# Four of six residual updates of the seven-product down projections sent through ScalarE and an accumulating transfer

## The chip, the core and the metric

The kernel runs on one core of a Trainium2 chip. A core has five engines that each work through a queue of their own in order: TensorE (PE in the profile; its weight loads are PEld), VectorE (DVE), ScalarE (ACT), GpSimd (POOL) and SyncE (SP). They wait for each other through semaphores, and 16 DMA engines move data beside them. The metric is the device time of one execution in microseconds, smaller is better.

## What is computed

A two-layer decoder trunk on 512 tokens of width 1024, all in float32. Each layer is a half-step feed-forward network, a mixer (gated linear attention in layer 0, stick-breaking attention in layer 1), and another half-step feed-forward network, so there are four feed-forward networks:

```
def swiglu(h, w_gate, w_up, w_down):
    return (jax.nn.silu(h @ w_gate) * (h @ w_up)) @ w_down

for i in range(DEPTH):                       # DEPTH = 2
    x = x + 0.5 * swiglu(rmsnorm(x, ffn1_norm[i]), ...)
    x = x + mixer(rmsnorm(x, mix_norm[i]))
    x = x + 0.5 * swiglu(rmsnorm(x, ffn2_norm[i]), ...)
return rmsnorm(x, final_norm)                # D_MODEL = 1024, D_FF = 2816, SEQ = 512
```

What the change touches is `x = x + 0.5 * (... @ w_down)`.

## The kernel before

**Data.** The residual x stays on the chip for the whole run as eight tiles `xs[0]` to `xs[7]`, 128 features by 512 tokens each (`x_81` to `x_88` in the order of instructions). To keep float32 accuracy, every operand of a product is split into a high part (`wh`, `hh`, ..., made by a cast on ScalarE, L538) and a low part (`wl`, `hl`, ..., made by a subtraction on VectorE, L539), and every product is three matmuls: high by high, low by high, high by low.

**Seven products.** The 2816 hidden features are cut into 11 slices of 256 and these into five groups; groups 1, 2 and 3 go through `seven_down`, a two-by-two block scheme with seven products in place of eight (Strassen's, in Winograd's form). The four output blocks of a pair of residual tiles `xs[m]` (lower) and `xs[m + 4]` (upper), each 128 by 256 (a half of the tokens), are (0,0), (0,1), (1,0) and (1,1): `up` picks the tile, `col` the half. One block of work (one m) runs seven products, each of 9 matmuls of 128 by 256 where the group has three slices (n = 3). They accumulate in three PSUM tiles, `ws` (ps_w), `zs` (ps_z) and `qs` (ps_q), and after each of six of the products a partial sum is added to a residual block:

| product (matrix name) | adds into PSUM | then updates x block |
|---|---|---|
| 1 b11 | ws (copied to zs by ScalarE, L843) | none |
| 2 t1 | qs | (1,1) from qs |
| 3 t2 | ws | (0,1) from ws |
| 4 b21 | zs | (0,0) from zs |
| 5 t3 | ws | (1,1) from ws |
| 6 b22 | qs | (0,1) from qs |
| 7 t4 | ws | (1,0) from ws |

Products 3, 5 and 7 add on top of the same `ws`, so each of them must wait until the value before it has been read out. Before, all six updates are `add`, one VectorE instruction `x = 0.5 * ps + x` (L831). For product 5 ScalarE first copies `ws` to a spare tile `u3` in SBUF (L869, `u` in the profile), so that product 7 can go on, and VectorE adds from the copy.

Each of four networks has three such groups of four values of m: 48 blocks, 288 updates. In the last network the third group has n = 2 and runs two m at a time (6 matmuls a product); the other 44 blocks are alike. The scheme for the gate and up products (`seven`, PE L1164) is of the same kind and shares the spare-tile tag `c`.

**Order.** The order on each engine is not that of the code. A `Planner` walks all instructions with a price for each, simulates the five queues and writes a fixed order for each engine. TensorE takes the first instruction in code order that can start within 30 ns, otherwise the one that can start soonest; VectorE and ScalarE take what is due first; POOL keeps the order of the code. A transfer is priced by these lines, as 2050 ns plus its bytes divided by 318 per ns (2462 ns for 128 KB):

```
        if "DMA" in kind:
            total = max((s[1] * s[3] for s in sizes), default=1) * 4
            return 2050.0 + total / 318.0, total / 318.0
```

POOL is nearly unused: some fills, and ten transfers (the gate weights `gr` and `w`, constants `tri`, `lf`, `negm`, the last norm's gain `fin`). All weights are loaded by transfers that SP issues (L504). Tiles of a tag are recycled among its `bufs` buffers: the writer of a tile waits until the last reader of the one that had the buffer is done.

Of the kernel before, what the change touches and what calls it, by code (L numbers as in the profile page):

```python
# [11 lines left out]
F32 = mybir.dt.float32  # L12
# [3 lines left out]
AF = mybir.ActivationFunctionType  # L16
ALU = mybir.AluOpType
PSUM = bass.MemoryType.PSUM

P = 128  # L20
# [409 lines left out]
def turns(t):  # L430

    return t.rearrange("p (two n) -> p n two", two=2)


def flat(ps):

    return ps.rearrange("p (n two) -> p two n", two=2)


def pair(t):  # L440

    return t.rearrange("p (two n) -> p two n", two=2)
# [3 lines left out]
def decoder(ctx: ExitStack, tc: tile.TileContext, a: dict, out: bass.AP):  # L446
    nc = tc.nc
# [12 lines left out]
    def psum(name, tag=None):  # L460
        if tag is None:
            tag = order[turn_[0] % 8]
            turn_[0] += 1
        return pp.tile([P, T], F32, tag=tag, bufs=banks[tag], name=name)
# [11 lines left out]
    xs = [xp.tile([P, T], F32, name=f"x{k}") for k in range(KD)]  # L476
# [311 lines left out]
    def seven_down(pool, w, r0, hs, part, n, per):  # L788

        H = T // 2
        W_ = per * P
        lower, upper = (
            Chunk(w[r0 : r0 + 2 * n * P, c : c + W_].rearrange("(f p) c -> p f c", p=P), 2 * n, W_)
            for c in (part * W_, 512 + part * W_)
        )
        lower.few = upper.few = True
        v = {}

        def halves():

            lo, up = (c.load().rearrange("p (c two) d -> p two c d", two=2) for c in (lower, upper))
            return lo[:, 0], lo[:, 1], up[:, 0], up[:, 1]

        def sums_12(_):
            a11, _, a21, a22 = halves()
            s = v["s12"] = pool().tile([P, 2 * n, W_], F32, tag="s", bufs=4, name="s12")
            nc.vector.tensor_tensor(out=s[:, 0:n], in0=a21, in1=a22, op=ALU.add)
            nc.vector.tensor_tensor(out=s[:, n:], in0=s[:, 0:n], in1=a11, op=ALU.subtract)  # L810
            return s

        def sums_34(_):
            a11, a12, a21, _ = halves()
            s = pool().tile([P, 2 * n, W_], F32, tag="s", bufs=4, name="s34")
            nc.vector.tensor_tensor(out=s[:, 0:n], in0=a11, in1=a21, op=ALU.subtract)
            nc.vector.tensor_tensor(out=s[:, n:], in0=a12, in1=v["s12"][:, n:], op=ALU.subtract)
            return s

        def prod(ps, w, k0, m, b, first):  # L820
            for c in range(n):
                bh, bl = (turns(t) for t in hs[c][b])
                wh, wl = (t[:, k0 + c, m * P : (m + 1) * P] for t in w)
                for i, (l_, r_) in enumerate(((wh, bh), (wl, bh), (wh, bl))):
                    nc.tensor.matmul(  # L825
                        ps, l_, r_, start=first and c + i == 0, stop=c == n - 1 and i == 2, skip_group_check=True
                    )

        def add(m, up, col, ps):
            x = pair(xs[part * per + m + 4 * up][:, col * H : col * H + H])  # L830
            nc.vector.scalar_tensor_tensor(out=x, in0=ps, scalar=0.5, in1=x, op0=ALU.mult, op1=ALU.add)  # L831

        def body_1(W):
            a11, s, v["a2"] = W
            ws, zs, qs = [], [], []
            for m in range(per):
                ws.append(psum("ps_w")[:, 0:H])
                prod(ws[m], a11, 0, m, "b11", True)
            for m in range(per):


                zs.append(psum("ps_z")[:, 0:H])
                nc.scalar.copy(zs[m], ws[m])  # L843
            yield

            ps = psum("ps_q")
            for m in range(per):
                qs.append(ps[:, m * H : (m + 1) * H])
                prod(qs[m], s, 0, m, "t1", m == 0)
            for m in range(per):  # L850
                add(m, 1, 1, flat(qs[m]))
            yield
            for m in range(per):
                prod(ws[m], s, n, m, "t2", False)
                add(m, 0, 1, flat(ws[m]))
            yield
            for m in range(per):
                prod(zs[m], v["a2"], 0, m, "b21", False)
                add(m, 0, 0, flat(zs[m]))
            v["w"], v["q"] = ws, qs  # L860
            yield

        def body_2(W):
            (s,) = W
            ws, qs = v["w"], v["q"]
            for m in range(per):
                prod(ws[m], s, 0, m, "t3", False)
                u3 = pool().tile([P, H], F32, tag="c", bufs=1, name="u3")
                nc.scalar.copy(pair(u3), flat(ws[m]))  # L869
                add(m, 1, 1, pair(u3))  # L870
            yield
            for m in range(per):
                prod(qs[m], s, n, m, "b22", False)
            for m in range(per):
                add(m, 0, 1, flat(qs[m]))
            yield
            for m in range(per):
                prod(ws[m], v["a2"], n, m, "t4", False)
                add(m, 1, 0, flat(ws[m]))
            yield  # L880

        units = [
            (lower, lambda t: halves()[0], n, W_),
            (lower, sums_12, 2 * n, W_),
            (lower, lambda t: halves()[1::2], 2 * n, W_),
        ]
        feed.q.append(Entry(units, body_1))
        feed.q.append(Entry([(lower, sums_34, 2 * n, W_)], body_2))

    def back_tok(w, r0, nf, hs, done):  # L890
# [160 lines left out]
    class FFN:  # L1051
# [87 lines left out]
        def seven(self, ch, group=None):  # L1139
# [4 lines left out]
            H = T // 2  # L1144
# [14 lines left out]
            def prod(o, w, w0, b, first=True, c0=0):  # L1159
                for j in range(4):  # L1160
                    bh, bl = (turns(t) for t in b(j))
                    wh, wl = (t[:, w0 + j, c0 : c0 + P] for t in w)
                    for n, (l_, r_) in enumerate(((wh, bh), (wl, bh), (wh, bl))):
                        st["pe"] = nc.tensor.matmul(  # L1164
                            o, l_, r_, start=first and j + n == 0, stop=j == 3 and n == 2, skip_group_check=True
                        ).ins

            def half(k0, c):
                return lambda j: (st["h"][k0 + j][:, c * H : c * H + H], st["l"][k0 + j][:, c * H : c * H + H])

            def gate(o, c, t):

                if group is None:
                    st["silu"] = nc.scalar.activation(pair(o[:, c : c + H]), t, AF.Silu).ins
                else:
                    g = self.gates[0 if o is v["o"][0] else 1]
                    nc.vector.tensor_tensor(
                        out=pair(o[:, c : c + H]), in0=t, in1=pair(g[:, c : c + H]), op=ALU.mult
                    )
# [23 lines left out]
            def body_2(W):  # L1203
                (s,) = W
                w, q = (v[n][:, 0:H] for n in "wq")
                o0, o1 = v["o"]
                prod(w, s, 0, lambda j: self.t_half(2, j), first=False)
                u3 = self.tp.tile([P, H], F32, tag="c", bufs=1, name="u3")
                nc.scalar.copy(pair(u3), flat(w))
                nc.vector.tensor_tensor(out=o1[:, H:T], in0=u3, in1=o1[:, H:T], op=ALU.add)  # L1210
                yield
                prod(q, s, 4, half(4, 1), first=False)
                oh = pair(o0[:, H:T])
                nc.vector.tensor_tensor(out=oh, in0=flat(q), in1=oh, op=ALU.add)
                gate(o0, H, oh)
                if group is not None:
                    close_0(o0)
                gate(o1, H, pair(o1[:, H:T]))
                yield
                prod(w, v["a2"], 0, lambda j: self.t_half(3, j), first=False, c0=P)  # L1220
                gate(o1, 0, flat(w))
                if group is not None:
                    close_1(o0, o1)
                    del self.gates[:2]
                else:
                    self.gates += [o0, o1]
                yield

            def close_0(o0):
                if group in self.DOWN_SEVEN:  # L1230
                    self.close_first(o0, group)
                else:
                    self.close(o0, group)

            def close_1(o0, o1):
                if group in self.DOWN_SEVEN:
                    self.close_second(o0, o1, group)
                else:
                    self.close(o1, group)
# [1121 lines left out]
```

## Time and profile before

| | |
|---|---|
| three runs | 1739.17, 1741.15, 1742.62 us; median 1741.15 |
| profiled execution | 1741.74 us, of which the span from the first to the last instruction is 1740.0 |
| granted TensorE clock | 0.999 |
| TensorE busy | 1729.9 us (99% of the span) |
| VectorE busy | 1618.7 us (93%) |
| ScalarE busy | 1142.1 us (66%) |
| POOL busy | 10.0 us |
| DMA | 179.35 MB, mean 103 GB/s |

Busy time of an engine is the time in which at least one of its instructions ran. Rows of the profile name the kernel's line, the engine, the operation, the tiles written and read and, after `x`, the count; a wait is put down to the instruction that ended it.

### The profile page before, as it was taken

To read this page: it belongs to the slowest core of one execution; us is meant where nothing else is said; L and a number is where in the kernel's file an instruction comes from. 1 tells how busy PE (TensorE), PEld (TensorE's weight loads), DVE (VectorE), ACT (ScalarE), POOL (GpSimd) and SP (SyncE) were. 2 spreads that over 40 slices of the span, in tenths; PEclk is the share of its full clock that TensorE was granted. 3 is DMA by queue.
4 is the path that set the end of the run, shared out by engine and by line. 5 is a ranking of instruction groups with operands and counts; after the bars stand their busy time and mean duration, and the time that the engine had idled before them with its cause. 6 is when DMAs were issued, how large, how long until landed. Compare 5 with 4: busy or idle time off the path is not lost.

```text
span 1740.0 us, 32878 instructions
## 1 busy us (share of the span) xinstructions
PE 1729.9 (99%) x13206; PEld 1633.0 (94%) x13206; DVE 1618.7 (93%) x2856; ACT 1142.1 (66%) x2056; POOL 10.0 (1%) x24
## 2 busy tenths in 40 slices
PE   9999999999999999999999999999999999999998
PEld 8999999988888999999989999999888888999997
DVE  8999999987888999999999999998898669999997
ACT  7666666664656766666677575657889757666655
POOL 0000000100000000000000000000000000000000
PEclk9999999999999999999999999999999999999999
DMA  6433333321223333333233333233222233333422
GB/s 187 134 101 119 104 116 107 97 95 51 73 98 106 115 106 115 101 119 110 92 115 122 108 112 119 89 105 88 62 73 76 72 106 115 110 110 110 122 87 81
DMA packets 209324, 179.35 MB, mean 103 GB/s; under 512 B 4434, under 2 KB 197252, under 8 KB 209172
## 3 DMA queue, kind: packets, MB, share of 16 engines
q1 hardware_dynamic: 208320, 175.91, 32.8%
q8 instruction: 103, 1.69, 0.4%
q0 software_dynamic: 608, 1.05, 0.2%
q14 instruction: 49, 0.40, 0.1%
q10 hardware_dynamic: 244, 0.29, 0.0%
HBM read 175.17 MB, written 2.10 MB: 102 GB/s over the span
## 4 chain that ended last, share of the span: by engine, by line
PE 91%; DVE 7%; ACT 1%; DMA 1%; issue 1%; DVEq 0%; ACTq 0%; SPq 0%
PE ps_w L1164 21%; PE ps_f L479 15%; PE ps_q L1164 10%; PE ps_w L825 10%; PE ps_q L825 5%; PE ps_z L1164 5%; PE ps_t L479 5%; PE ps_b L479 4%; PE ps_d L479 4%; PE ps_z L825 3%; DVE wl L539 2%; PE ps_z L1849 2%; PE ps_oT L1934 1%; PE ps_T L1919 1%; PE ps_bt L479 1%; PE ps_S L479 1%
## 5 line engine op out<-in xcount | busy, mean ns | idle before, releaser
L538 ACT CAST wh<-s 128x1024 fp32r<-128x1024 f32 (+1 forms) x236 | 229.2, 971 | 113.4 <-PE ps_q L1164 28.1
L539 DVE TENSOR_TENSOR wl<-raw,wh 128x1024 fp32r<-128x1024 f32 x241 | 254.1, 1056 | 31.3 <-ACT wh L538 31.1
L539 DVE TENSOR_TENSOR wl<-s,wh 128x1024 fp32r<-128x1024 f32 (+1 forms) x236 | 263.1, 1115 | 1.6 <-ACT wh L538 1.4
L538 ACT CAST wh<-raw 128x1024 fp32r<-128x1024 f32 x241 | 221.3, 921 | 58.5 <-PE ps_b L479 20.7
L1164 PE MATMUL ps_w<-th,wh 128*128 128x256 f32 x864 | 238.0, 275 | 0.0
L1164 PE MATMUL ps_w<-th,wl 128*128 128x256 f32 x864 | 237.6, 275 | 0.0
L1164 PE MATMUL ps_w<-tl,wh 128*128 128x256 f32 x864 | 237.6, 275 | 0.0
L479 PE MATMUL ps_f<-xh,wh 128*128 128x512 f32 x432 | 166.7, 386 | 0.0
L1164 PEld LDWEIGHTS ps_w<-th,wh 128*128 128x128 f32 x864 | 165.8, 192 | 0.4 <-ACT o L1197 0.2
L1164 PEld LDWEIGHTS ps_w<-tl,wh 128*128 128x128 f32 x864 | 165.9, 192 | 0.0
L1164 PEld LDWEIGHTS ps_w<-th,wl 128*128 128x128 f32 x864 | 165.9, 192 | 0.0
L479 PE MATMUL ps_f<-xh,wl 128*128 128x512 f32 x432 | 163.7, 379 | 0.0
L479 PE MATMUL ps_f<-xl,wh 128*128 128x512 f32 x432 | 163.7, 379 | 0.0
L539 DVE TENSOR_TENSOR wl<-rawd,wh 128x384 fp32r<-128x384 f32 (+2 forms) x152 | 92.6, 614 | 1.1 <-ACT wh L538 1.1
L479 PEld LDWEIGHTS ps_f<-xl,wh 128*128 128x128 f32 x432 | 81.6, 189 | 12.1 <-DVE xl L941 0.2
L479 PEld LDWEIGHTS ps_f<-xh,wh 128*128 128x128 f32 x432 | 81.7, 189 | 11.0
L479 PEld LDWEIGHTS ps_f<-xh,wl 128*128 128x128 f32 x432 | 81.7, 189 | 10.7
L825 PE MATMUL ps_w<-hh,wh 128*128 128x256 f32 x324 | 90.5, 279 | 0.0
L825 PE MATMUL ps_w<-hh,wl 128*128 128x256 f32 x324 | 89.1, 275 | 0.0
L825 PE MATMUL ps_w<-hl,wh 128*128 128x256 f32 x324 | 89.1, 275 | 0.0
L538 ACT CAST wh<-rawd 128x384 fp32r<-128x384 f32 (+2 forms) x152 | 84.6, 566 | 4.1 <-PE ps_f L479 1.8
L1164 PE MATMUL ps_w<-nh,wl 128*128 128x256 f32 x288 | 79.2, 275 | 0.0
(353 smaller groups left out, 5747.2 us busy)
## 6 DMA issues: line engine op xcount, KB each, us to landing
raw<-in_ffn_w_gate_dram SPq DMA_DIRECT2D x43, 1024.0 KB, 5.4
raw<-in_ffn_w_up_dram SPq DMA_DIRECT2D x43, 1024.0 KB, 5.3
rawd<-in_ffn_w_down_dram SPq DMA_DIRECT2D x88, 384.0 KB, 3.5
raw<-in_gla_w_in_dram SPq DMA_DIRECT2D x12, 1024.0 KB, 5.2
rawd<-in_ffn_w_down_dram SPq DMA_DIRECT2D x18, 512.0 KB, 3.7
raw<-in_sb_w_in_dram SPq DMA_DIRECT2D x16, 512.0 KB, 4.0
raw<-in_gla_w_out_dram SPq DMA_DIRECT2D x4, 1024.0 KB, 5.0
raw<-in_sb_w_in_dram SPq DMA_DIRECT2D x4, 1024.0 KB, 5.2
```

Source lines behind the costliest of these rows:

```text
L479: nc.tensor.matmul(ps, l, r, start=first, stop=last, skip_group_check=seeded)
L538: nc.scalar.copy(h[:, k], part)
L539: nc.vector.tensor_tensor(out=l[:, k], in0=part, in1=h[:, k].bitcast(F32), op=ALU.subtract)
L825: nc.tensor.matmul(ps, l_, r_, start=first and c + i == 0, stop=c == n - 1 and i == 2, skip_group_check=True)
L1164: st["pe"] = nc.tensor.matmul(o, l_, r_, start=first and j + n == 0, stop=j == 3 and n == 2, skip_group_check=True).ins
L1849: nc.tensor.matmul(o_, l_, r_, start=first, stop=last, skip_group_check=True)
L1919: nc.tensor.transpose(ps[:, c0 : c0 + P], ys[yb][:, yc + j * P : yc + (j + 1) * P], ident)
L1934: nc.tensor.matmul(po[e * 64 : e * 64 + 64, j * P : T], self.v[j][:, c : c + 64], self.wt[p, e][bk][:, c0 : c0 + n], start=j == 0, stop=j ...
```

## The change

A new helper `send` stands beside `add`: ScalarE copies half of the PSUM value to a spare tile `c` of 128 by 256, and POOL issues a transfer from that tile onto the residual block which adds (`accum_op=ALU.add`). Four of the six updates use it: after products 3, 4, 5 and 7. Those after products 2 and 6 (from `qs`) stay on VectorE. The tag `c` gets two buffers in place of one, for `u3` in `seven` too. In the changed kernel `send` is L835 (copy) and L836 (transfer), and lines below move down by 3 to 5.

```diff
+        def send(m, up, col, ps):
+            t = pool().tile([P, H], F32, tag="c", bufs=2, name="c")
+            nc.scalar.activation(pair(t), ps, AF.Copy, scale=0.5)
+            nc.gpsimd.dma_start(xs[part * per + m + 4 * up][:, col * H : col * H + H], t, accum_op=ALU.add)
...
                 prod(ws[m], s, n, m, "t2", False)
-                add(m, 0, 1, flat(ws[m]))
+                send(m, 0, 1, flat(ws[m]))
...
                 prod(zs[m], v["a2"], 0, m, "b21", False)
-                add(m, 0, 0, flat(zs[m]))
+                send(m, 0, 0, flat(zs[m]))
...
                 prod(ws[m], s, 0, m, "t3", False)
-                u3 = pool().tile([P, H], F32, tag="c", bufs=1, name="u3")
-                nc.scalar.copy(pair(u3), flat(ws[m]))
-                add(m, 1, 1, pair(u3))
+                send(m, 1, 1, flat(ws[m]))
...
                 prod(ws[m], v["a2"], n, m, "t4", False)
-                add(m, 1, 0, flat(ws[m]))
+                send(m, 1, 0, flat(ws[m]))
...
-                u3 = self.tp.tile([P, H], F32, tag="c", bufs=1, name="u3")
+                u3 = self.tp.tile([P, H], F32, tag="c", bufs=2, name="u3")
```

The planner then writes other orders. In the first block of the first group, `ws` is ps_w_1430 and `qs` is ps_q_1442. On TensorE product 7 follows product 6 before:

```order
L825 MATMUL ps_q_1442<-hh_1287,wl_1374 128x256
L825 MATMUL ps_q_1442<-hl_1288,wh_1373 128x256
L825 MATMUL ps_w_1430<-hh_641,wh_1367 128x256
L825 MATMUL ps_w_1430<-hh_641,wl_1368 128x256
L825 MATMUL ps_w_1430<-hl_642,wh_1367 128x256
```

and now, where ps_w_1539 is the `ws` of the next block:

```order
L825 MATMUL ps_q_1442<-hl_1288,wh_1373 128x256
L825 MATMUL ps_w_1539<-nh_341,wh_1477 128x256
L825 MATMUL ps_w_1539<-nh_341,wl_1478 128x256
L825 MATMUL ps_w_1539<-nl_342,wh_1477 128x256
L825 MATMUL ps_w_1539<-nh_398,wh_1477 128x256
L825 MATMUL ps_w_1539<-nh_398,wl_1478 128x256
L825 MATMUL ps_w_1539<-nl_399,wh_1477 128x256
L825 MATMUL ps_w_1430<-hh_641,wh_1367 128x256
```

Six of the next block's nine first matmuls now stand ahead of product 7. In 30 of the 44 alike blocks it is five, in eleven six or seven, and in the other three five longer ones of 512 columns. In the last network's third group the rows are mixed more freely.

On ScalarE, at the same place, before (u3_1507 is the copy after product 5, ps_z_1440 is `zs`):

```order
L843 COPY ps_z_1440<-ps_w_1430 128x256
L538 CAST wh_1473<-rawd_1235 128x384
L1174 ACTIVATE o1_1306<-o1_1306 128x256
L869 COPY u3_1507<-ps_w_1430 128x256
L538 CAST wh_1477<-s12_1379 128x768
```

and now, from the second send of the block on:

```order
L835 ACTIVATE c_1474<-ps_z_1440 128x256
L538 CAST wh_1481<-s12_1379 128x768
L538 CAST wh_1485<-rawd_1235 128x384
L538 CAST wh_1485<-rawd_1377 128x384
L835 ACTIVATE c_1511<-ps_w_1430 128x256
L538 CAST wh_1491<-s34_1427 128x768
```

The third send (c_1511) takes the buffer that the first had, and three weight casts now stand between the second and the third. Those of the next block's s34 weights stand behind the third.

On VectorE before (x0_81 is the lower residual tile, x4_85 the upper):

```order
L831 SCALAR_TENSOR_TENSOR x4_85<-u3_1507,x4_85 128x256
L831 SCALAR_TENSOR_TENSOR x0_81<-ps_z_1440,x0_81 128x256
L539 TENSOR_TENSOR wl_1478<-s12_1379,wh_1477 128x768
L539 TENSOR_TENSOR wl_1482<-rawd_1235,wh_1481 128x384
L539 TENSOR_TENSOR wl_1488<-s34_1427,wh_1487 128x768
```

and now:

```order
L539 TENSOR_TENSOR wl_1482<-s12_1379,wh_1481 128x768
L539 TENSOR_TENSOR wl_1486<-rawd_1235,wh_1485 128x384
L539 TENSOR_TENSOR wl_1486<-rawd_1377,wh_1485 128x384
L831 SCALAR_TENSOR_TENSOR x0_81<-ps_q_1442,x0_81 128x256
L539 TENSOR_TENSOR wl_1492<-s34_1427,wh_1491 128x768
```

The update after product 6 writes the block that the first send has added to, so it waits for that transfer; the next block's s34 weights (wl_1492) are queued behind it. POOL now issues 192 transfers, and `gr`, which was its first, stands behind the first 48 of them, `fin` behind all.

## Prediction

> **What bounds the kernel now.** I read the busy times at the head of the page first, then the waits of TensorE, then the stretch of the first seven-product group.
>
> ```profile
> span 1740.0 us, 32878 instructions
> PE 1729.9 (99%) x13206; PEld 1633.0 (94%) x13206; DVE 1618.7 (93%) x2856; ACT 1142.1 (66%) x2056; POOL 10.0 (1%) x24
> ```
>
> ```profile
> PE ps_f L2135 <- DVE gT L471: 0.9, 1, 0.9
> PE ps_R L994 <- DVE dg L990: 0.7, 1, 0.7
> PE ps_f L479 <- DVE nl L1262: 0.4, 1, 0.4
> PE ps_f L479 <- ACT nh L1261: 0.3, 1, 0.3
> PE ps_on L479 <- ACT sh L1681: 0.3, 1, 0.3
> ```
>
> ```profile
> 111.00:139.20 28.20, 28.20 (x254) 28.16 (x253) 28.00 (x58) 15.34 (x31) 0.00 (x0) 1.00 0.38 111
> ```
>
> TensorE is busy for 1729.9 of 1740.0 us, and the five waits in the second fence (us in total, times, longest) are all that it has: 2.6 us in 1740. The third fence is the table by stretches for the first group's four blocks; its columns are length, TensorE, weight loads, VectorE, ScalarE and POOL busy, clock, DMA share, GB/s. VectorE is full there (28.00 of 28.20), and yet TensorE lacks nothing. So VectorE is a nearly full engine that is never late, and the bound is TensorE. The next fence shows how dense it is (start, duration), and where the copy of the old kernel falls:
>
> ```profile
> 116.01 0.28 PE L825 MATMUL ps_w<-hl,wh 128*128 128x256 f32 x1
> ...
> 117.13 0.28 PE L825 MATMUL ps_w<-hh,wh 128*128 128x256 f32 x1
> ```
>
> ```profile
> 116.36 0.38 ACT L869 COPY u<-ps_w 128x256 f32<-128x256 f32 x1 [2.22 <-PE ps_w L825]
> ```
>
> The first row is the last matmul of product 5, the second the first of product 7, with the nine of product 6 between: ten steps in 1.12 us, 0.112 each. A product of nine is 1.01 us and a block of seven 7.06. The copy starts 0.35 after the start of the last matmul of its product, which is 0.07 after its end (0.28), and takes 0.38. I use 0.07 for every hand-over by a semaphore.
>
> **What the change removes.** Four VectorE updates a block, 48 blocks:
>
> ```profile
> L831 DVE SCALAR_TENSOR_TENSOR x<-ps_q,x 128x256 f32<-128x256 f32 x96 | 39.5, 413 | 0.1
> L831 DVE SCALAR_TENSOR_TENSOR x<-ps_w,x 128x256 f32<-128x256 f32 x96 | 38.9, 413 | 0.6 <-PE ps_w L825 0.5
> ...
> L831 DVE SCALAR_TENSOR_TENSOR x<-u,x 128x256 f32<-128x256 f32 x48 | 19.9, 415 | 0.0
> L831 DVE SCALAR_TENSOR_TENSOR x<-ps_z,x 128x256 f32<-128x256 f32 x48 | 19.8, 414 | 0.4
> ```
>
> The ps_w, u and ps_z rows go: 38.9 + 19.9 + 19.8 = 78.6 us of VectorE, 1.66 us of every block's 7.06. TensorE waits for none of it, so this is worth at most the 2.6 us of all waits, most of which stand outside these blocks. I take 0.
>
> **What it adds on ScalarE.** Three more copies a block, 144 in all, at 0.38: 55 us on an engine that is busy 15.34 of 28.20 in the stretch. By itself this is hidden in its idle time, and the term is 0; what counts is when each copy may start.
>
> **What it adds on POOL.** 192 transfers.
>
> ```profile
> 317.07 1.94 POOL L1476 DMA_DIRECT2D w<-in_gla_w_gk_dram  x4 [0.30 <-POOL w L1474]
> ```
>
> Four issues took 1.94 us, 0.49 each; four a block are 2.0 of 7.06 us, so POOL keeps up. What it is moved past: `gr` now goes out behind 48 sends and `fin` behind all.
>
> ```profile
> L1467 ACT CAST gs<-gr x1: 280/280/280, 335.1 to 335.1; 128x128 fp32r<-128x128 f32 x1
> ```
>
> ```profile
> L2010 DVE TENSOR_SCALAR fin<-fin x1: 680/680/680, 1706.4 to 1706.4; 128x1024 f32<-128x1024 f32 x1
> ```
>
> `gr` is first read at 335.1. Its group's last product ends near 320; the send, `gr`'s issue and its slow landing (5.0, below) reach about 329, so some 6 us remain. `fin` is read at 1706.4, far enough behind the last group too. Both 0.
>
> **What it makes wait.** This is the term that decides. The third send of a block (after product 5) reuses the buffer of the first (after product 3), so its copy waits until the first transfer has landed; and product 7 accumulates on the `ws` that this copy reads, so TensorE waits for the copy. Count from the start of the last matmul of product 3: 0.35 until the first copy starts, 0.38 the copy, 0.07 to POOL, L from issue to landing, 0.07 back to ScalarE, 0.38 the third copy, 0.07 to TensorE: 1.32 + L. Against it stands what the new order puts between: one step to the end, products 4, 5 and 6 with 27 steps, and the next block's matmuls. With five of them it is 33 steps, 3.70 us; with six, 3.81. So TensorE loses nothing up to L = 2.38 in the 30 blocks with five, up to 2.49 in the other 14 of this kind, and above that every microsecond of L is a microsecond of each block. The second copy and three weight casts stand ahead of the third copy on ScalarE; the rows behind the old copy show at what spacing such instructions start:
>
> ```profile
> 116.63 0.83 ACT L538 CAST wh<-s 128x768 fp32r<-128x768 f32 x1
> 117.37 0.51 ACT L538 CAST wh<-rawd 128x384 fp32r<-128x384 f32 x1
> 117.78 0.85 ACT L538 CAST wh<-s 128x768 fp32r<-128x768 f32 x1
> ```
>
> 0.27 after a copy, 0.74 after a cast of 768 columns, 0.41 after one of 384. The second copy can start at 1.01 + 0.35, so the third is free of them at 1.36 + 0.27 + 0.74 + 2 x 0.41 = 3.19, just before the 0.87 + 2.38 = 3.25 at which TensorE begins to lose. So the landing binds, not the casts.
>
> **What L is.** No row shows an adding transfer. The nearest rows (KB, us from issue to landing):
>
> ```profile
> out_dram<-x SPq DMA_DIRECT2D x2, 128.0 KB, 2.0
> ...
> lf<-in_c_lvl_dram POOLq DMA_DIRECT2D x1, 224.0 KB, 2.6
> ...
> gr<-in_gla_w_in_dram POOLq DMA_DIRECT2D x1, 64.0 KB, 5.0
> tri<-in_c_tri_dram POOLq DMA_DIRECT2D x1, 64.0 KB, 2.0
> ```
>
> Lower end: the plain store of the same 128 KB from the chip's memory, 2.0. POOL's own line from 64 KB (2.0) to 224 KB (2.6) gives 2.24 for 128 KB in one pass. An update must fetch the old x as well as the copy, two reads; at 256 KB the same line gives 2.72. Upper end: `gr`, 5.0 for 64 KB in small pieces, if every row of an adding transfer were as slow. The rows of a send are 1 KB long, like those of `lf` (1.75 KB) and unlike `gr`'s 64 bytes, so I go by `lf` and `tri` with two reads, 2.72. The weights' loads share the DMA engines:
>
> ```profile
> rawd<-in_ffn_w_down_dram SPq DMA_DIRECT2D x1, 384.0 KB, 3.2
> ```
>
> ```profile
> rawd<-in_ffn_w_down_dram SPq DMA_DIRECT2D x1, 384.0 KB, 4.1
> ```
>
> The first was issued at 119.0 alone, the second at 120.3 behind it: a meeting cost 0.9. Loads fill 0.38 of the stretch, so a send pays 0.34 if each meeting cost as much; it is smaller and meets them only in part, and I take 0.1. L = 2.82.
>
> A page speaks against a cost here. The Trainium skill, DMA: Bandwidth & Descriptors, section "Anatomy of one DMA — SWDGE (gpsimd) path", gives a transfer of POOL's as 2.0 us plus bytes over 436e3 per us, an estimate of 2.30 for 128 KB, and by it nothing would wait; `tri` and `lf` agree with it within 0.15, but neither adds. The page Collectives: The Full Stack, section "The bandwidth ceiling", says that an add in the DMA engines costs not cycles but two source reads; by both, an estimate of 2.6, the sum would be 9 us. No row here shows which holds.
>
> **The sum.** 30 x (2.82 - 2.38) + 14 x (2.82 - 2.49) = 13.2 + 4.6 = 17.8 us. The last network's third group sends eight pairs through the two buffers with less between them; at 0.44 each, 3.5. Together 21 us, on the profiled execution's 1741.74 (span 1740.0 and 1.7 around it) 1763; the median of the runs shown is 0.6 lower, so I predict 1762.
>
> VectorE gets a wait too: the update after product 6 needs the first landing, at 0.87 + L = 3.69, where its product is ready at 28 steps + 0.35 = 3.49. These 0.2 us stop the queue behind it, above all the split of the next block's s34 weights, which TensorE first needs in that block's product 5; VectorE has been freed of 1.66 us in each block, so I cost it at 0. If L passed 5 that cover would be gone. The last blocks of a network have product rows of the fifth group behind them before the residual is normed, which covers their landing.
>
> **The rivals.**
> 1. No wait: the adding transfer lands within 2.4 us, the one-pass line. For it: 2.0 and 2.24 above; against it: the second read and the loads. Then nothing in the sum is left: 1741, within 0.2% (3.5 us, about what a measurement of this kernel can tell from no change). It decides below L = 2.46, where the sum passes 3.5.
> 2. A long landing: each row's two reads, add and write go one after the other. For it: `gr`, where many small pieces took 5.0; against it, the length of the rows. L = 3.4 gives 30 x 1.02 + 14 x 0.91 + 8 x 1.02 = 51, 1793; L = 4.0 gives 48.6 + 21.1 + 13 = 83, 1824; L = 5.0, 134, 1875. Above about 3.6 the next block's first copy also waits, for the third landing, and adds to it.
> 3. VectorE's relief pays: 78.6 us less on a 93% busy engine lets TensorE run without its waits. For it: VectorE 28.00 of 28.20 in the stretch; against it: 2.6 us of waits in the whole span. At best 1738, which is still not 0.2%.
>
> **Chances.** Rival 1 0.26, my forecast (L from 2.46 to 3.4, 1745 to 1793) 0.49, rival 2 0.21, rival 3 or an unseen gain 0.04. Faster by over 0.2% 0.03, within 0.2% 0.27, slower 0.70. The range holds rivals 1 and 3's upper part, my forecast and rival 2 up to L = 4: 1739 to 1820, leaving out about 0.15.
>
> **What the profile after should show.** The issues by line: 192 of 128 KB from POOL with about 2.8 us to landing. VectorE's busy time near 1540, ScalarE's near 1197. Among the waits, ScalarE's L835 for a DMA in every block, and TensorE's ps_w L825 for L835, some 20 us in all, between products 6 and 7. If that group is missing and L is below 2.4, rival 1 was right. If L is right and TensorE still does not wait, my chain or the count of steps is wrong; if TensorE waits at L539, the wait of VectorE was not covered.

## The result and the profile after

The changed kernel takes 1847.58 us (median of four runs, 1842.18 to 1855.95), the kernel before beside it 1740.16. The ratio is 1.0619 with a 95% interval of 1.0571 to 1.0668: 6% slower. The direction was foreseen, the size was not: 107 us where the prediction had 21, and above the upper end of its range. The profiled execution is the shortest of the four (1842.18, granted clock 0.995); in the two longest the granted clock is 0.991 and 0.990.

The head of the page after, and TensorE's waits (us in total, times, longest):

```profile
span 1840.4 us, 33326 instructions
PE 1753.4 (95%) x13206; PEld 1641.5 (89%) x13206; DVE 1574.4 (86%) x2664; ACT 1191.1 (65%) x2200; POOL 175.4 (10%) x216
```

```profile
PE ps_w L825 <- ACT c L835: 38.8, 49, 2.1
PE ps_w L825 <- ACT ps_z L848: 28.0, 24, 3.7
PE ps_w L1167 <- ACT ps_z L1194: 10.6, 5, 4.6
```

VectorE was relieved (1618.7 to 1574.4 us busy), ScalarE took its copies (1191, as foreseen), and TensorE, which had 2.6 us of waits, now has some 77 us in three groups, 78 waits. The first group is for the greater part the predicted one: in 42 of its 49 waits (28.4 us) product 7 waits for the third send's copy. In the other seven (10.4 us) product 5 waits for the first send's copy, which the prediction had only for landings above 3.6. The other two groups were not predicted: TensorE waits for `ps_z L848` and `L1194`, copies that the change did not touch. They stand at the start of the next block, or of the gate and up products that follow a group.

What ScalarE and VectorE wait for, and the transfers (KB, median us from issue to landing):

```profile
ACT c L835 <- DMA x<-c: 170.7, 96, 5.4
```

```profile
DVE wl L539 <- ACT wh L538: 126.4, 139, 5.8
DVE x L831 <- DMA x<-c: 35.7, 22, 2.5
```

```profile
x<-c POOLq DMA_DIRECT2D x192, 128.0 KB, 3.3
```

More than half of the 192 copies wait for a landing, and not the third of each block alone: 10 first, 21 second, 45 third and 38 fourth ones started within 0.15 us behind the landing that frees their buffer. The median landing is 3.3 us, the longest 7.2.

One block shows both kinds of wait. ScalarE's rows in the first block of the second group (start, duration; in brackets the idle time before and what ended it), and the matmul that waits at the end:

```profile
209.54 0.38 ACT L835 ACTIVATE c<-ps_w 128x256 f32<-128x256 f32 x1
209.82 0.92 ACT L538 CAST wh<-rawd 128x384 fp32r<-128x384 f32 x2
210.64 0.39 ACT L835 ACTIVATE c<-ps_z 128x256 f32<-128x256 f32 x1
213.09 0.38 ACT L835 ACTIVATE c<-ps_w 128x256 f32<-128x256 f32 x1 [2.07 <-DMA x<-c]
213.37 0.82 ACT L538 CAST wh<-s 128x768 fp32r<-128x768 f32 x1
216.28 0.38 ACT L835 ACTIVATE c<-ps_w 128x256 f32<-128x256 f32 x1 [2.08 <-PE ps_q L825]
216.56 0.38 ACT L848 COPY ps_z<-ps_w 128x256 f32<-128x256 f32 x1
```

```profile
216.99 0.38 PE L825 MATMUL ps_w<-hh,wh 128*128 128x256 f32 x1 [0.74 <-ACT ps_z L848]
```

The four L835 rows are the sends after products 3, 4, 5 and 7. The third waits 2.07 us for the first to land: that is the predicted wait. The fourth reuses the buffer of the second, which was issued at 211.32 and landed after 4.86 us at 216.18; the copy starts 0.10 behind that. (The row names a matmul as what ended the wait. But of the 125 copies that started within 0.3 us of the landing that frees their buffer, 105 started 0.104 or 0.105 behind it, and 216.18 + 0.10 is this start.) Right behind the fourth copy in ScalarE's queue stands L848 of the next block, its copy of product 1 to `zs`, and the next block's product 3 may not add to `ws` before that copy has read it. So a late second landing stops TensorE a block later, by way of an instruction that has nothing to do with the send.

This holds throughout. Followed back along ScalarE's queue, all 78 waits of the three groups lead to a copy that started 0.08 to 0.11 us behind the landing two sends before it, with no more than 0.1 us of idle time of ScalarE at any step between. Behind 28 of the 29 waits for L848 and L1194 it is a fourth copy.

Counted from the start of each matmul to the next over the dense step, TensorE's gaps sum to 6.7 us before and 97.0 after; the rest of the longer span is mostly a lower clock (below). By place: 39.7 us ahead of product 7, the predicted kind (35.3 of them right behind a third copy; a gap ahead of product 5 is among the rest), and 51.9 us in what comes next (30.9 between products 2 and 3 of the next block, 9.5 between its products 4 and 5, 11.5 in the gate and up products that follow a group).

### The profile page after: what moved, and what is told of

It is laid out like the page before. It is cut to its first block, busy times and chain, and to the rows that moved or that the text cites. A ratio compares the mean times of both kernels' runs of the same rounds, so it can differ in the third digit from the quotient of the medians.

```text
span 1840.4 us, 33326 instructions
## 1 busy us (share of the span) xinstructions
PE 1753.4 (95%) x13206; PEld 1641.5 (89%) x13206; DVE 1574.4 (86%) x2664; ACT 1191.1 (65%) x2200; POOL 175.4 (10%) x216
## 4 chain that ended last, share of the span: by engine, by line
issue 40%; PE 3%; POOL 3%; DVE 2%; DMA 1%; ACT 1%; POOLq 0%; DVEq 0%; ACTq 0%
POOL x L836 3%; DMA x<-c 1%; DVE wl L539 1%; PE ps_w L1167 1%; PE ps_bt L479 1%; PE ps_q L1167 0%; PE ps_w L825 0%; PE ps_z L1167 0%; ACT wh L538 0%; PE ps_T L2019 0%; ACT c L835 0%; DVE hl L1265 0%; DVE ts L1343 0%; DVE x L2031 0%; PE ps_d L479 0%
## 5 line engine op out<-in xcount | busy, mean ns | idle before, releaser
L836 POOL DMA_DIRECT2D x<-c x192 | 165.5, 866 | 1524.6 <-ACT c L835 1317.3
L539 DVE TENSOR_TENSOR wl<-s,wh 128x1024 fp32r<-128x1024 f32 (+1 forms) x236 | 263.4, 1119 | 51.9 <-ACT wh L538 50.9
L1167 PE MATMUL ps_w<-th,wh 128*128 128x256 f32 x864 | 239.0, 277 | 10.7 <-ACT ps_z L1194 10.6
L835 ACT ACTIVATE c<-ps_w 128x256 f32<-128x256 f32 x144 | 55.3, 384 | 191.4 <-DMA x<-c 157.3
L825 PE MATMUL ps_w<-hh,wh 128*128 128x256 f32 x324 | 98.0, 303 | 67.2 <-ACT c L835 38.8
L825 PEld LDWEIGHTS ps_w<-hh,wh 128*128 128x128 f32 x324 | 62.4, 193 | 82.8 <-ACT c L835 49.7
```

The costliest lines, as they stand in the source:

```text
L539: nc.vector.tensor_tensor(out=l[:, k], in0=part, in1=h[:, k].bitcast(F32), op=ALU.subtract)
L825: nc.tensor.matmul(ps, l_, r_, start=first and c + i == 0, stop=c == n - 1 and i == 2, skip_group_check=True)
L835: nc.scalar.activation(pair(t), ps, AF.Copy, scale=0.5)
L836: nc.gpsimd.dma_start(xs[part * per + m + 4 * up][:, col * H : col * H + H], t, accum_op=ALU.add)
L1167: st["pe"] = nc.tensor.matmul(o, l_, r_, start=first and j + n == 0, stop=j == 3 and n == 2, skip_group_check=True).ins
```

## The theories

A: the landings. A send takes much longer where it meets weight loads, and each copy waits for the landing two sends back, so ScalarE's whole queue stands still. B: VectorE's update after product 6 waits for the first landing and holds up the weight splits behind it. C: ScalarE's added copies themselves. D: the adding transfer is slow in itself.

## Experiments

### The transfers alone

The model is left out; only transfers run, in groups such as

```diff
+        for _ in range(5):  # add 128 1024
+            ready(big)
+            nc.sync.dma_start(big, gate)
+            nc.gpsimd.dma_start(dst[:, 0:256], src[:, 0:256], accum_op=ALU.add)
```

> The disputed cost by itself: this kernel leaves out the model and only runs transfers one after the other, each waiting for the one before, five of each kind: plain and adding transfers between two tiles on the chip of 64, 128 and 256 KB issued by POOL, then adding ones of 128 KB issued together with one weight load of 384 KB, with two, and with one of 1024 KB. In the changed kernel the sends landed after 2.6 us at best, 3.3 in the median, 7.2 at worst. Theory A (a send queues behind the weight loads in flight): adding 128 KB alone 2.65, plain 128 KB alone about 2.2, together with one load of 384 KB about 4.5, with two about 5.5, with one of 1024 KB about 7, that is a little after the load itself lands. Rival (the adding transfer itself is erratic or slow in a crowded queue of its own): spread from 2.6 to 5 already alone, and a load adds 0.5 us at most, as engines share packet by packet.

The lone adding transfer of 128 KB (min, median, max of five), then two that were issued just behind a load of 384 KB and of 1 MB (SyncE runs ahead of the groups, so the load can be that of a later one, here L74):

```profile
DMA to landing us min/median/max: 2.6/2.7/2.7
```

```profile
la<-in_ffn_w_down_dram SPq DMA_DIRECT2D x1, 384.0 KB, 3.3
dst<-src POOLq DMA_DIRECT2D x1, 128.0 KB, 3.5
```

```profile
218.99 0.37 SPq L74 DMA_DIRECT2D big<-in_ffn_w_gate_dram  x1
219.24 0.85 POOL L71 DMA_DIRECT2D dst<-src  x1 [5.84 <-DVE big L31]
```

```profile
big<-in_ffn_w_gate_dram SPq DMA_DIRECT2D x1, 1024.0 KB, 5.7
dst<-src POOLq DMA_DIRECT2D x1, 128.0 KB, 6.0
```

The last send was issued 0.25 us behind its load and landed 0.5 us after it (225.21 against 224.74). The transfer does not share the way with the load in proportion to its 128 KB; it lands when the load has landed. Plain transfers behind a 1 MB load took 5.4 to 5.6, so this is no matter of the add. The Trainium skill, DMA: Bandwidth & Descriptors, section "Queues, rings and completion order", says that each DMA engine goes round-robin between its queues, a packet at a time; by that rule alone a short transfer would pass a long one. Here it did not.

Nor is it the completion alone that comes late. A lone send's first packet moved 1.43 us after the start of its issue; this one's moved 4.41 after it, when the load's last packet was 0.5 us away, and VectorE was idle all the while. A plain 128 KB transfer that ScalarE issued 0.02 us ahead of such a load landed after 4.5 to 4.6 us, 1.3 before the load, so there the two did mix.

Of the expectation, the lone 2.65 held; behind loads both sends were sooner than the 4.5 and 7 of theory A, and far beyond the half microsecond of its rival.

### Fewer load buffers, more copy buffers

A buffer of `c` takes 1 KB a partition. In these runs the room for more of them comes from one buffer of the loaded down weights (tag `rawd`). The kernel before with `rawd` in two buffers is the control:

```diff
-tag="rawd", bufs=3
+tag="rawd", bufs=2
```

> A control: the kernel before with two buffers in place of three for the loads of the down weights, which frees the 4 KB that the next run uses. All theories: 1740 to 1750, since the loads are prefetched several products ahead; if it is much slower, the next run has to be read against it.

1769.61, ratio 1.0167 [1.0152, 1.0182], more than expected: the third load buffer is worth 1.7% by itself. Against this control, the change with two, three and six buffers of `c`:

> The changed kernel with rawd in two buffers in place of three and c still in two: the partner that was missing for the kernel with six buffers of c and two of rawd (1781, its own control without sends 1770). Theory A: c's buffers are the bulk, so with two of them the loss over the control is again 90 to 110: 1850 to 1880, and the step from six buffers to two is 70 to 100. Theory B (VectorE waits for landings, whatever c has): no more than 1790. If fewer loads in flight shorten the landings, A comes out at 1830 to 1850.

> rawd in two buffers as in its control (1770 without sends, 1844 with sends and two buffers of c, 1781 with six), c in three. A copy then waits for the landing of the send three before it, about 1.2 to 3 us further back. Theory A: only landings beyond about 4 to 5 us still delay TensorE, so most of the 63 us between two and six buffers are back: 1785 to 1800. If the landing must be covered by a whole block's distance (because sends pile up behind the same load), 1800 to 1825.

> The changed kernel with six buffers for the copies (and two for the loads, as in the control), so that no copy waits for a transfer that is less than some 9 us old; the updates after product 6 still wait for the first transfer of their block. Theory A (the copies wait for a buffer whose transfer has not landed, and ScalarE's queue stands still behind them): within 0.5% of the control, 1740 to 1755. Theory B (VectorE waits for the landing in the updates after product 6, and the weight splits behind it come late): still 1820 or more. Theory C (the extra copies on ScalarE): still 1820 or more.

1844.15, 1782.40 and 1781.28: over the control 74.5, 12.8 and 11.7 us. One more buffer takes back 62 us, further ones nothing. TensorE's waits in the three groups with two buffers of `c`, then with three:

```profile
PE ps_w L825 <- ACT c L835: 55.6, 58, 3.7
PE ps_w L1167 <- ACT ps_z L1194: 5.3, 4, 2.5
PE ps_w L825 <- ACT ps_z L848: 2.2, 3, 0.8
```

```profile
PE ps_w L825 <- ACT c L835: 10.6, 18, 1.6
PE ps_w L825 <- ACT ps_z L848: 5.0, 8, 1.0
PE ps_w L1167 <- ACT ps_z L1194: 2.9, 3, 1.7
```

The landings are no shorter there than with two (median 3.7 against 3.1) or in the change (3.3), yet the three groups fall from 63.1 to 18.5 us. So the wait for a buffer of `c` is the bulk, and A holds. About half of the 18.5 still leads back to a landing; most of the rest leads to a weight cast that waits for VectorE's sums. With two, the loss over the control is below the 90 to 110 expected and the time in the range given for shorter landings. Six and three buffers end near each other: three slightly below the 1785 expected of it, six 0.7% above the control, where A had expected less than 0.5% and no more than 1755.

### The copies without the transfers

```diff
-            nc.gpsimd.dma_start(xs[...][...], t, accum_op=ALU.add)
+            nc.vector.tensor_tensor(out=x, in0=t, in1=x, op=ALU.add)
```

> The four updates go by the same ScalarE copy with the same two buffers, but VectorE adds from the copy in place of the transfer: no transfer at all, 144 more copies than before, VectorE as full as before. Theories A and B: 1740 to 1755, as no wait for a landing is left. Theory C (the copies themselves, and the other order that they make): 1800 or more.

1745.08, ratio 1.0023 [1.0014, 1.0033]. All of ScalarE's copies and the two buffers, with VectorE adding from the copy, cost some 4 us; C is small.

### The add and the loads, apart and together

Three kernels and a control. The transfer without `accum_op`; the change with the parts of a group sharing one set of down weights, which takes away six of eight loads of a group; both; and the kernel before with few loads.

```diff
-            nc.gpsimd.dma_start(..., t, accum_op=ALU.add)
+            nc.gpsimd.dma_start(..., t)
```

```diff
+        if part == 0:
+            once[:] = [Chunk(w[...]) for c in (0, 512)]
+        lower, upper = once
```

> The changed kernel with the adding transfer made a plain one: the copy overwrites the residual block, so the add itself is left out, everything else (192 transfers, buffers, order) stays. Theory A (a send behind a weight load lands only with that load, whether it adds or not): a lone transfer gets 0.7 us faster (1.95 for 2.66), but those behind loads still take 3 to 6, so most of the loss stays: 1795 to 1825. Rival D (the add's second read is what is long): with every transfer at 1.95 to 2.3 nothing waits, 1741 to 1750. Theory B (VectorE waits for landings) expects little else than A.

> The changed kernel with all four parts of a group using part 0's down-projection weights, so that six of eight loads of a seven-product group are gone (the other parts' weights are left out of the computation). Theory A: nearly every send is alone and lands at 2.66, above the 2.38 and 2.49 of the sum in the prediction: 30 x 0.28 + 14 x 0.17 = 11 us and some for the blocks that still meet a load: 1750 to 1765 where its own control is at 1740. Rival D (the adding transfer is long or slow in itself, loads or not): 1820 to 1850 as with the full loads.

> Control of the one with few loads: the kernel before with the same weights left out. It waits for nothing now, so all theories expect 1738 to 1742.

> Few loads (all parts of a group use part 0's weights, the others' are left out) and the plain transfer (the add is left out too). A lone plain transfer lands at 1.97, below the 2.12 at which TensorE would begin to wait with the measured hand-overs (0.293 from the copy's end to POOL, 0.104 from the landing to the next copy). If lengths of landings are all of it, the third copies cost nothing and only the 40 or so sends that meet a load cost something: 12 to 22 us over the control's 1737.6, that is 1750 to 1760. If the two effects simply add (43 for loads with a plain transfer, 64 for the add with few loads, 107 for both), about 0 is left: 1738 to 1745. If some other cost of the sends were at work (POOL's issues, the order), 1770 or more.

| | time (us) | over its control | gaps ahead of product 7 | gaps in the next block |
|---|---|---|---|---|
| adding, all loads (the change) | 1847.6 | 107 | 39.7 | 51.9 |
| adding, few loads | 1801.2 | 64 | 36.4 | 16.9 |
| plain, all loads | 1785.1 | 43 | 10.6 | 33.7 |
| plain, few loads | 1767.6 | 30 | 8.8 | 14.7 |

Controls are 1740.2 beside the change, 1742.1 beside the plain transfer, and 1737.6 for few loads (1738 to 1742 expected). The ratios of the last three rows to the kernel before are 1.0336 [1.0321, 1.0351], 1.0250 [1.0228, 1.0271] and 1.0158 [1.0141, 1.0174]. The gap columns go by the matmuls on both sides of a gap, so a few us of the first gap column are ahead of product 5. Neither A alone nor D alone is right, and the expectations of the pure cases (1795 and more for plain, 1765 and less for few loads) were missed. The columns show why: the two kinds of gap have two causes. Ahead of product 7 the lone length of a landing decides, and the loads hardly matter. In the next block the loads matter most (51.9 to 16.9), and the add too (51.9 to 33.7).

The first is seen in one block with few loads, where the send meets nothing (last matmul of product 3, copy, POOL's issue, third copy, first matmul of product 7):

```profile
120.49 0.28 PE L829 MATMUL ps_w<-hl,wh 128*128 128x256 f32 x1
...
120.85 0.38 ACT L839 ACTIVATE c<-ps_w 128x256 f32<-128x256 f32 x1 [0.22 <-ACT o L1181]
...
121.53 0.85 POOL L840 DMA_DIRECT2D x<-c  x1 [1.60 <-ACT c L839]
...
124.29 0.38 ACT L839 ACTIVATE c<-ps_w 128x256 f32<-128x256 f32 x1 [1.95 <-DMA x<-c]
...
124.73 0.38 PE L829 MATMUL ps_w<-hh,wh 128*128 128x256 f32 x1 [0.39 <-ACT c L839]
```

The copy ends at 121.23 and POOL begins 0.30 later. That step is 0.292 to 0.294 in 183 of the 192 sends, in the change, here and with the plain transfer. The send lands after 2.66 at 124.19, the copy follows after 0.10. From the first row to the last it is 4.24 us = 1.58 + 2.66. The 33 steps between take 3.70, so TensorE loses 0.54 with a landing that meets nothing, and nothing only up to L = 2.12. A lone plain transfer takes 1.97, which is why the column falls from 40 to 11 without the add.

The few loads with the plain transfer were expected at 1750 to 1760 and took 1767.6. Their gaps, 29.5 in all of which 6.6 are in the control, are close; what the expectation lacked is, by this sum, the clock, 0.995 where the control has 0.999, some 7 us.

### Which sends matter

Two sends a block (after 4 and 7), two others (after 3 and 5), and one (after 7), the rest on VectorE as before:

```diff
-                send(m, 0, 1, flat(ws[m]))
+                add(m, 0, 1, flat(ws[m]))
```

> Only the updates after products 4 and 7 go by transfers, from two buffers; those after 2, 3, 5 and 6 stay on VectorE (that after 5 through a copy in the same tag c, as before). The buffer is then used three times a block instead of four, and no VectorE update in the block reads a block that a send of the same product chain has just written. Theory A: the tile c is still passed around, a landing of 3 to 6 us meets one that is needed again about a block's half later: 1755 to 1785. Theory B (VectorE update after product 6 behind the first send): that wait is gone, so if B were the bulk, 1741 to 1750. Theory C (copies): 2 to 3 us.

> Only the updates after products 3 and 5 go by transfers, so each has a buffer of its own and its next use is a block later; those after 2, 4, 6 and 7 stay on VectorE. The update after product 6 still writes the block that the first send adds to, so VectorE waits for that landing as in the change. Theory A (buffer waits): nothing is left of the loss but a few rare landings, 1742 to 1750. Theory B (VectorE's wait behind the landing): its share shows alone; in the kernel with six buffers what was left was 11 us with 31 us of VectorE waits, so 1750 to 1765.

> Only the update after product 7 goes by a transfer; the other five stay on VectorE (that after 5 through u3 in the same tag, two buffers). Nothing in the same block reads the block again or needs the buffer within half a block. Theory A and B both: 1741 to 1746, a landing of 3 to 7 us is then covered. If it loses more than 8 us, landings as such (their time on the DMA engines, POOL, the longer loads) cost TensorE something without a wait for a buffer.

1751.64 (1.0052 [1.0037, 1.0067]), 1749.93 (1.0053 [1.0038, 1.0068]) and 1740.77 (1.0002 [0.9992, 1.0012]). The first fell between its two expectations; its largest wait of TensorE, 4.3 us in 8 times, is for the copy after product 5 (`u` L874), each time behind a send's landing. The second was to show B alone. VectorE still waits there for 13 landings, but of TensorE's waits 6.4 us are for a copy:

```profile
DVE s L809 <- DMA rawd<-in_ffn_w_down_dram: 16.0, 21, 2.8
DVE x L831 <- DMA x<-c: 11.0, 13, 1.6
```

```profile
PE ps_w L825 <- ACT c L835: 6.4, 8, 1.2
...
PE ps_q L825 <- DVE wl L539: 0.7, 1, 0.7
PE ps_q L825 <- DVE x L831: 0.6, 1, 0.6
```

None of the eight waits for a copy leads back to a buffer or a send's landing. In each the copy stood behind a weight cast that waited for VectorE's sum, and in seven VectorE had itself waited 0.6 to 2.8 us for a weight load to land (16.0 us of such waits in all, 1.7 in the kernel before, 1.0 in the change). So late loads are a third cost, small here; whether the sends slow the loads or the new order issues them later was not separated. B's own part is 1.3 us there. In the kernel with six buffers TensorE waited 6.2 us for `x L831`, so B is real and small; in the change itself none of TensorE's waits is for that update. One send a block costs nothing, though its landing has a median of 4.1: nobody needs its buffer or its block of x for a whole block.

### An order that knows the landing

The planner's price of the transfer, 2462 ns, set to 5000 and to 3300:

```diff
+            if e == "Pool" and total == 131072:
+                return 5000.0, total / 318.0
```

> The changed kernel with one number changed: the planner prices a 128 KB transfer of POOL's at 5000 ns where it had 2462. It then puts 24 to 28 matmuls more between products 6 and 7 in most blocks (33 to 37 where there were 14), so that the chain from send to send is covered up to a landing of about 4.3 to 4.6 us. Theory A: the waits between products 6 and 7 fall to those of the longest landings, 1775 to 1805; the pulled-forward matmuls need their weights earlier, which may cost some. Rival E (the order is not what is short, ScalarE's queue or the landings behind loads stop TensorE elsewhere): 1820 to 1850 still.

> The planner prices a 128 KB transfer of POOL's at 3300 ns, the measured median: 7 to 12 matmuls more between products 6 and 7 in most blocks (21 to 26 where there were 14). Covered are landings up to about 2.9 to 3.4. If 5000 overshot, this is clearly below 1832: 1780 to 1815. If an order written for one length cannot cover landings that lie between 2.7 and 7: 1815 to 1845.

1832.02 (1.0527 [1.0504, 1.0550]) and 1839.09 (1.0580 [1.0541, 1.0619]). The first fell in the range of rival E, and the second ended likewise, so 5000 did not overshoot, and neither order takes the loss away. TensorE's waits at 5000:

```profile
PE ps_q L827 <- DVE wl L541: 7.8, 10, 3.3
PE ps_w L1169 <- ACT ps_z L1196: 7.5, 8, 2.6
PE ps_w L827 <- ACT c L837: 6.9, 7, 2.6
PE ps_w L1169 <- ACT u L1214: 6.3, 7, 1.4
PE ps_q L827 <- ACT wh L540: 4.2, 6, 2.2
PE ps_w L1169 <- DVE wl L541: 4.2, 8, 1.7
```

The predicted wait is nearly gone (6.9 where it was 38.8), and about as much waits elsewhere (all gaps still sum to some 76 us): for weight casts and splits that now come too late, for copies behind them, and for copies behind a landing. At 3300 TensorE waits 46.4 us for copies of L837, and nearly all of it leads back to a landing; but 33.9 of it is for the first copy of a block and 11.3 for the third, where the change has 10.4 and 28.4. Both orders shrink the predicted wait, and others take its place.

## Why the prediction was too low

- **The bound** (TensorE, VectorE's relief worth nothing) was right. No kernel with sends ran faster than the kernel before.
- **The mechanism** was right for the one wait that was priced: third copy, first landing, product 7. The wait stands in the trace where it was put.
- **The length of a lone adding transfer** was right, in part by luck: 2.72 taken, as two reads on the line of POOL's loads, 2.66 measured. On the chip a plain transfer of 128 KB took 1.95 where that line has 2.24, and one of 256 KB, the bytes of two reads, 2.27 where it has 2.72. The Trainium skill, Collectives: The Full Stack, section "The bandwidth ceiling", has an add cost two source reads. The growth with size agrees: from 64 to 256 KB the adding transfer grew by 0.92 and the plain one by 0.48. But two reads on the measured line end near 2.3; part of what remains is POOL's longer issue, since the first packet of a lone adding transfer moves at 1.43 and of a plain one at 1.11. (At the 2.6 of that estimate the prediction's own sum gives 10 us and not 9.)
- **First term that failed: "I use 0.07 for every hand-over by a semaphore."** From a copy's end to POOL's issue it is 0.293, from a landing to ScalarE 0.104. The chain is 1.58 + L and not 1.32 + L, the threshold 2.12 and not 2.38. Over the 44 blocks that is some 11 us. The first sends themselves had L = 2.79 (median), next to the 2.82 taken, though only three of the 44 met a load at their issue; the lone length is 2.66. The excess of their landings over 2.12 sums to 35.7 us, and the gaps right behind a third copy to 35.3. Predicted were 21.
- **Second, and larger: "a send pays 0.34 if each meeting cost as much; it is smaller and meets them only in part, and I take 0.1."** One L was made for all sends from the mean share of loads, but the loads have a phase. They go out when VectorE and ScalarE have read a weight tile, at about the second and third send. A weight load had been issued and not landed when the issue began of 3 of 44 first sends, 25 second, 41 third and 21 fourth ones, and the medians are 2.79, 4.68, 4.25 and 3.02 us. Three other waits open with these, and the prediction had them shut, since "above about 3.6 the next block's first copy also waits" was tested with 2.82. They are worth 51.9 us.
- **The place of these waits** was seen for the first copy only. That the fourth copy waits for the second landing, and that the next block's L848 is queued behind it, was missed: ScalarE was costed by its idle time, not by what stands behind a waiting instruction.
- **VectorE's wait at 0** was right for the change, where TensorE has no wait for it; with two sends it is 1.3 us, with six buffers 6.2. VectorE's busy time came to 1574 and not 1540. Nearly all of the 34 us is overlap: the durations of all rows fell by 75 us, but neighbouring rows overlap (an update lasts 0.41 and the next row starts 0.33 behind it), and busy time counts that once.
- **POOL** keeps up as foreseen, though an issue takes 0.86 us and not 0.49.
- **Rival 2** had the size (1824 at L = 4.0, 1875 at 5.0) from a landing that is long by itself. That condition did not come true, the lone landing is 2.66; the size came out there by another way.

## What to carry to other kernels

A new wait in an in-order queue is priced by every instruction behind it, not by the idle time of its engine; follow each reuse of a buffer to its writer and then to what is queued behind that writer. Take the length of a transfer at the phase at which it will be issued, against the loads that go out there, and not from a mean share of the DMA engines. Before moving work to a transfer, ask how many sends lie between a buffer's uses: here two cost 75 us over the control, three 13, and one send a block nothing.

## What the hardware showed that was not expected

A 128 KB transfer that POOL issues 0.25 us behind a 1 MB load lands with it, adding or plain: an adding one 0.5 to 0.6 us behind the load, a plain one 0.05 to 0.16 before it. An adding transfer holds POOL for 0.86 us, a plain one for 0.54.

A long wait costs more than itself. In the first group of the changed kernel (columns as in the prediction's table):

```profile
151.16 0.58 PE L1167 MATMUL ps_w<-th,wh 128*128 128x256 f32 x1 [4.57 <-ACT ps_z L1194]
151.53 0.42 PE L1167 MATMUL ps_w<-th,wl 128*128 128x256 f32 x1
151.75 0.42 PE L1167 MATMUL ps_w<-tl,wh 128*128 128x256 f32 x1
```

```profile
111.00:151.00 40.00, 30.94 (x263) 29.60 (x262) 27.85 (x49) 20.29 (x42) 13.84 (x16) 1.00 0.70 149
151.00:155.00 4.00, 3.84 (x21) 3.85 (x22) 2.89 (x4) 1.79 (x5) 0.05 (x1) 0.59 0.23 33
```

After 4.57 us without work the steps are 0.21 instead of 0.11 for 3 us, and the granted clock of that stretch is 0.59: another 1.5 us. The Trainium skill, TensorE: Matmul & The Clock Gate, section "What's actually happening", has the clock halved after an idle window of about 3.4 us and restored after as long a busy one; this stretch agrees.

The span has three more such stretches, each of 3.41 us at a granted clock of 0.50, from 1041.7, 1222.6 and 1782.4 on; the kernel before has none until its last matmul. The length is about that of the Trainium skill's window, but two of them did not need an idle window: the longest waits just ahead of the three are 3.7, 2.0 and 2.1 us, and before the last two TensorE was busy for 0.41 and 0.37 of 3.41 us. So waits of 2 us were enough here. Four such stretches at half speed are some 7 us, which is what the mean clock of 0.995 where it was 0.999 comes to.
